# A transformer block with experts on one core: the last expert group and its norm in one pass of tokens, and the context's second-layer products moved behind it

## The chip, the cores and the metric

The kernel runs on one core of a Trainium2 chip. The metric is device microseconds of one execution. Engines: PE is TensorE (matmuls; its weight loads are listed as PEld), DVE is VectorE, ACT ScalarE, POOL GpSimd, SP SyncE (it only issues transfers here). Every time below is in us unless marked ns.

## What is computed

512 tokens of 1024 numbers pass through two blocks in float32. The first has a mixer (retention and spatial gating) and 16384 experts, of which each token takes the 16 best of each of 8 heads:

```python
expert = k1 * PEER_N_KEYS + k2
g = jax.nn.softmax(top_s.astype(jnp.float32), axis=-1).astype(hb.dtype)
ue = expert_u[expert]
act = jax.nn.gelu(jnp.einsum('td,thkd->thk', hb, ue), approximate=False) * g
ve = expert_v[expert]
return jnp.einsum('thk,thkd->td', act, ve)
...
x = x + gate2[:, None, :] * peer(h2, ...)
return rms_norm(x, final_g)
```

The second block has two layers. Each takes x and a context of 256 tokens, both normed and modulated, through one wide product; then window attention and latent attention (each over the tokens and the context), a gated convolution and a merge. Layer 0 also updates the context, `mixer_layer(..., update_ctx=(i < DEPTH_2 - 1))`; of the context, layer 1 uses only keys and values: the latent `kvlb` (256 wide), which is normed, `kr` (32), `ka` (128) and `va` (128).

## The kernel before

Every float32 product is three products of split operands (`mm3`, lines 81 to 85: high by high, low by high, high by low). So each weight tile is loaded (SP, `wr`), its high part cast on ACT (line 108, `wh`), and its low part subtracted on POOL or DVE (line 110, `wl`).

**Experts** (`experts`, line 563). For 384 tokens all experts are computed. *Up products*: for each block of 128 experts 24 products of 128x384 into `u`; the result leaves through ACT (`hb`, line 739) for memory (`hd`). Two accumulators `u` take turns. These blocks are handed out by the generator `units`, in part as filler between the steps of the routing and of the context's layers. *Down products*: 32 groups of 4 rows of 128 experts; for each row `vr` is loaded and split (`vh`, `vl`), `at` = `ht` x `gt` (line 626) is the gated activation and is split (`ah`, `al`), and 24 products of 128x384 add to eight accumulators `acc`. For the last 128 tokens only the chosen experts are computed: 128 steps, each of which gathers rows (`sg<-ur,xid` and `sg<-ev,xid`, issued by POOL), takes a dot product on DVE (line 200, via `htok`) and adds into `sacc` (line 723). `self.sparse(n)` hands these steps out by the weights S3, S4, SU and S5, which are steps per piece of dense work.

**Context** (`context`, line 1382). It runs while up products last, for both layers of the second block: the norm, the products (`cm`), in layer 0 the attention, the convolution and the merge; then the updated context is stored (`cxd`), loaded again for layer 1, normed, and its keys and values are stored to `cd[1]`.

**The last group and the norm** (`first_out`, line 903). Group 31 is computed in two halves of tokens, 256 and then 256 of which 128 come from `sacc` by a transpose (line 649). After each half: squares on ACT, sums by small products (`cs,sq`, line 928), a root on DVE, a broadcast by PE (line 159), and the modulated and split input `hh`, `hl` of layer 0.

The order of instructions within an engine is made by a scheduling layer from the program text, so code that is written in another place moves the instructions of all engines and the transfers in SP's queue.

Of the kernel before, what the change touches and what calls it, by code (L numbers as in the profile page):

```python
# [8 lines left out]
F32 = mybir.dt.float32  # L9
# [21 lines left out]
S3, S4, SU, S5 = 0.8, 0.95, 1.2, 0.82  # L31
# [24 lines left out]

class Kern:
# [23 lines left out]
    def mm3(self, ps, lh, ll, rh, rl, first, last):  # L81
        mm = self.nc.tensor.matmul
        mm(ps, lh, rh, start=first, stop=False)  # L83
        mm(ps, lh, rl, start=False, stop=False)  # L84
        mm(ps, ll, rh, start=False, stop=last)  # L85
# [167 lines left out]
    def build(self):  # L253
# [25 lines left out]
        self.cxd = dr.tile([128, 8, TC], F32, name="cxd")  # L279
        self.ud = [dr.tile([128, T], F32, name="ud%d" % k) for k in range(8)]  # L280
# [282 lines left out]
    def experts(self):  # L563
        nc, a, h = self.nc, self.a, self.h
        self.fine = ("",)
        with ExitStack() as s1:
# [21 lines left out]
            self.context(wc, pc, tick)  # L588
# [12 lines left out]
            self.last_units = True  # L601
# [5 lines left out]
            self.load(x, self.x1d)  # L607
# [3 lines left out]
            def update(c, lo, hi):  # L611
                nc.vector.scalar_tensor_tensor(x[:, c, lo:hi], acc[c][:, lo:hi], self.mod[:, 40 + c:41 + c], x[:, c, lo:hi],
                                               op0=OP.mult, op1=OP.add)
# [28 lines left out]
            def last(lo, hi):  # L642
                for c in range(8):
                    cs = slice(c * 128, (c + 1) * 128)
                    e = min(hi, TD)
                    for q, (vh, vl, ah, al) in enumerate(ops):
                        self.mm3(acc[c][:, lo:e], vh[:, cs], vl[:, cs], ah[:, lo:e], al[:, lo:e], q == 0, q == 3)
                    if hi > TD:
                        nc.tensor.transpose(acc[c][:, TD:T], self.sacc[:, cs], self.ident)
                    update(c, lo, hi)  # L650
                if hi == T and "x2" in self.dbg:
                    self.load(self.dbg["x2"], x)
# [249 lines left out]

    def first_out(self, scope, last, banks):
# [3 lines left out]
        turn = iter([banks[i] for i in (7, 6, 5, 1, 2, 3, 4, 1)])  # L907

        def stp():
            return next(turn)  # L910

# [8 lines left out]
        for hf, (lo, hi) in enumerate(HALVES):  # L920
            w = hi - lo
            last(lo, hi)
            sps = stp()
            for k in range(8):
                sq = p0.tile([128, w], F32, name="sq", tag="sq", bufs=3)
                nc.scalar.square(sq, x[:, k, lo:hi])
                for i in range(2):
                    nc.tensor.matmul(sps[:, 2 * i:2 * i + 2], sq[:, i * 128:(i + 1) * 128], cs[:, k, :],
                                     start=k == 0 and i == 0, stop=k == 7 and i == 1)
            sv = sps[:, :4].rearrange("p (i w) -> p w i", w=2)  # L930
            v = self.small.tile([128, 2, 2], F32, name="v2", tag="v2")
# [920 lines left out]
```

## Time and profile before

| | us |
|---|---|
| median of three runs | 3726.02 |
| lowest and highest | 3725.82, 3735.67 |
| the profiled execution | 3726.69 |
| its span | 3724.9 |
| PE, DVE, ACT, POOL busy | 3434.7, 2367.6, 1566.5, 1398.7 |
| last of the context's layer-0 products | 1667 |
| first down product | 1776.33 |
| first product of group 31 | 2293.51 |
| first window score of layer 0 | 2397.39 |

Busy times are sums over the whole span and overlap. The four points in time are from the trace and part the program into stages. Where a window of the trace is shown, the column PEclk is the mean granted clock of PE, with 1.00 for 2.4 GHz and 0.50 for 1.2 GHz.

### The profile page before, as it was taken

What the parts mean: (1) busy time and instruction counts of PE and PEld (TensorE: products, weight loads), DVE (VectorE), ACT (ScalarE), POOL (GpSimd) and SP (SyncE); (2) the same over time, 40 slices, a digit from 0 to 9 for tenths busy, and PEclk for the clock granted to TensorE, in tenths of its full rate; (3) what the DMA queues carried; (4) which work ended last, traced back from release to release, by engine and by line L of the source; (5) the groups of instructions that cost most, each with busy time, mean ns of one, the idle gap of its engine ahead of it and who ended that gap; (6) DMA issues with size and microseconds to landing.
All of it is one profiled execution on the core that took longest, in us unless ns stands there. A gap on an engine that the chain in (4) does not pass through costs nothing.

```text
span 3724.9 us, 54819 instructions
## 1 busy us (share of the span) xinstructions
PE 3434.7 (92%) x20315; PEld 3095.9 (83%) x20315; DVE 2367.6 (64%) x4607; ACT 1566.5 (42%) x2945; POOL 1398.7 (38%) x1170
## 2 busy tenths in 40 slices
PE   6999999978888988896999999899999988999998
PEld 5889788977788978896999999878878787787787
DVE  7876865698867666665777776444245664433554
ACT  3323233325653474643333333344346544442663
POOL 2210114452336667564222210455425335542442
PEclk9999999989999998998999998899999999999999
DMA  7667644337877757585999994322211422222123
GB/s 276 214 205 256 224 153 156 111 124 274 295 254 266 273 198 261 178 275 217 358 344 319 328 329 140 101 71 69 77 59 50 142 73 69 71 69 70 54 71 100
DMA packets 271948, 667.93 MB, mean 179 GB/s; under 512 B 25280, under 2 KB 87104, under 8 KB 268736
## 3 DMA queue, kind: packets, MB, share of 16 engines
q1 hardware_dynamic: 219248, 469.30, 37.5%
q0 software_dynamic: 36864, 134.23, 10.2%
q10 hardware_dynamic: 15568, 60.89, 4.2%
q8 instruction: 160, 2.62, 0.3%
q14 instruction: 108, 0.88, 0.1%
HBM read 601.34 MB, written 62.98 MB: 178 GB/s over the span
## 4 chain that ended last, share of the span: by engine, by line
PE 45%; DVE 4%; ACT 3%; DMA 3%; issue 2%; POOL 2%; SPq 0%; POOLq 0%; ACTq 0%; DVEq 0%
PE acc L85 5%; PE acc L84 5%; PE acc L83 5%; PE gm L83 3%; PE gm L84 3%; PE gm L85 3%; PE mm L83 3%; PE mm L85 3%; PE mm L84 3%; PE pv L1104 2%; PE tp L1074 2%; DMA vr<-ev 1%; PE sc L83 1%; PE sc L85 1%; PE sc L84 1%
## 5 line engine op out<-in xcount | busy, mean ns | idle before, releaser
L110 POOL TENSOR_TENSOR wl<-wr,wh 128x512 fp32r<-128x512 f32 (+2 forms) x348 | 483.6, 1406 | 350.6 <-ACT wh L108 325.5
L108 ACT CAST wh<-wr 128x512 fp32r<-128x512 f32 (+4 forms) x536 | 350.7, 667 | 560.7 <-PE mm L84 208.7
L83 PE MATMUL u<-hh,wh 128*128 128x384 f32 (+1 forms) x1040 | 362.6, 349 | 34.4 <-ACT hb L739 34.4
L85 PE MATMUL u<-hh,wl 128*128 128x384 f32 (+1 forms) x1040 | 360.5, 347 | 10.0 <-DVE wl L110 9.4
L84 PE MATMUL u<-hl,wh 128*128 128x384 f32 (+1 forms) x1040 | 359.8, 346 | 0.0
L84 PE MATMUL acc<-al,vh 128*128 128x384 f32 (+2 forms) x1056 | 353.4, 335 | 1.0 <-DVE al L110 1.0
L85 PE MATMUL acc<-ah,vl 128*128 128x384 f32 (+2 forms) x1056 | 353.4, 335 | 0.0
L83 PE MATMUL acc<-ah,vh 128*128 128x384 f32 (+2 forms) x1056 | 353.0, 335 | 0.0
L708 POOL DMA_INDIRECT sg<-ev,xid x128 | 158.0, 1234 | 313.5 <-DVE sacc L723 258.7
L108 ACT CAST vh<-vr 128x1024 fp32r<-128x1024 f32 x128 | 134.6, 1052 | 316.5 <-issue 140.3
L83 PE MATMUL mm<-hh,wh 128*128 128x512 f32 (+2 forms) x608 | 241.4, 401 | 8.5 <-DVE sm L419 4.2
L708 POOL DMA_INDIRECT sg<-ur,xid x128 | 145.2, 1135 | 276.9 <-DVE sg L200 260.1
L84 PE MATMUL mm<-hl,wh 128*128 128x512 f32 (+2 forms) x608 | 241.7, 398 | 7.4 <-POOL hl L110 5.4
L85 PE MATMUL mm<-hh,wl 128*128 128x512 f32 (+2 forms) x608 | 240.9, 396 | 4.4 <-DVE wl L110 4.4
L110 DVE TENSOR_TENSOR wl<-wr,wh 128x1024 fp32r<-128x1024 f32 (+4 forms) x188 | 179.5, 971 | 102.0 <-ACT wh L108 101.1
L110 DVE TENSOR_TENSOR vl<-vr,vh 128x1024 fp32r<-128x1024 f32 x128 | 159.6, 1247 | 127.3 <-ACT vh L108 124.8
L83 PEld LDWEIGHTS u<-hh,wh 128*128 128x128 f32 x1040 | 203.9, 196 | 36.6 <-ACT hb L739 35.3
L85 PEld LDWEIGHTS u<-hh,wl 128*128 128x128 f32 x1040 | 203.7, 196 | 12.9 <-DVE wl L110 12.0
L84 PEld LDWEIGHTS u<-hl,wh 128*128 128x128 f32 x1040 | 204.2, 196 | 0.3
L84 PEld LDWEIGHTS acc<-al,vh 128*128 128x128 f32 x1056 | 202.6, 192 | 1.4 <-DVE al L110 1.3
L85 PEld LDWEIGHTS acc<-ah,vl 128*128 128x128 f32 x1056 | 202.8, 192 | 0.0
L83 PEld LDWEIGHTS acc<-ah,vh 128*128 128x128 f32 x1056 | 202.5, 192 | 0.2 <-ACT hb L739 0.2
(723 smaller groups left out, 9936.9 us busy)
## 6 DMA issues: line engine op xcount, KB each, us to landing
wr<-eu SPq DMA_DIRECT2D x256, 256.0 KB
vr<-ev SPq DMA_DIRECT2D x128, 512.0 KB
wm<-wmod SPq DMA_DIRECT2D x88, 512.0 KB
wrc<-w SPq DMA_DIRECT2D x83, 512.0 KB
wr<-wA SPq DMA_DIRECT2D x80, 512.0 KB
wr<-w SPq DMA_DIRECT2D x156, 256.0 KB
wrg<-w SPq DMA_DIRECT2D x104, 256.0 KB
hd<-hb ACTq DMA_DIRECT2D x64, 384.0 KB
```

What stands on the lines that cost most here:

```text
L83: mm(ps, lh, rh, start=first, stop=False)
L84: mm(ps, lh, rl, start=False, stop=False)
L85: mm(ps, ll, rh, start=False, stop=last)
L108: nc.scalar.copy(hi, x)
L110: eng.tensor_tensor(lo, x, hi.bitcast(F32), op=OP.subtract)
L708: self.here(nc.gpsimd.indirect_dma_start(t, None, tabs[i], bass.IndirectOffsetOnAxis(idx[:, j:j + 1], 0)))
L1074: nc.tensor.transpose(t[:, (b - i) * 128:(b - i + 1) * 128], p[:, b * 128:(b + 1) * 128], self.ident)
L1104: nc.tensor.matmul(o[:, lo:hi], v(b), pt[k][:, b, lo:hi], start=i == 0 and k == 0, stop=i == len(parts) - 1 and k == 1)
```

## The change

The context's second layer leaves `context`: only the sums of its norm are still taken there, behind the merge, with up products between them (`unit`), and the row of roots is stored (`crd`). Its five products go into a new generator `context_last`, which `first_out` steps through. `first_out` takes group 31 in one pass over all 512 tokens. `mm3` and others keep the written order where `self.pinned` is set. The accumulators stay open from group 30 to group 31, so that the update of x behind group 30 goes. The load of x is written in the eighth group. S5 rises. The norm of layer 1's context latent moves to the window part of layer 1.

```diff
-S3, S4, SU, S5 = 0.8, 0.95, 1.2, 0.82
+S3, S4, SU, S5 = 0.8, 0.95, 1.2, 0.88
...
     def mm3(self, ps, lh, ll, rh, rl, first, last):
+        for i, (l, r) in enumerate(((lh, rh), (lh, rl), (ll, rh))):
+            ins = self.nc.tensor.matmul(ps, l, r, start=first and i == 0, stop=last and i == 2)
+            if self.pinned:
+                self.here(ins)
...
-            self.context(wc, pc, tick)
+            def unit(n=1):
+                for _ in range(n):
+                    self.sparse(SU)
+                    next(units, None)
+
+            self.context(wc, pc, tick, unit)
...
-            self.load(x, self.x1d)
...
+                if g == 8:
+                    self.load(x, self.x1d)
...
-                            self.mm3(acc[c][:, :TD], vh[:, cs], vl[:, cs], ah, al, g == 0 and q == 0, g == 30 and q == 3)
+                            self.mm3(acc[c][:, :TD], vh[:, cs], vl[:, cs], ah, al, g == 0 and q == 0, False)
                     self.sparse(S5)
-                if g == 30:
-                    for c in range(8):
-                        update(c, 0, TD)
...
+            def last(c):
+                cs = slice(c * 128, (c + 1) * 128)
+                for q, (vh, vl, ah, al) in enumerate(ops):
+                    self.mm3(acc[c][:, :TD], vh[:, cs], vl[:, cs], ah, al, False, q == 3)
+                self.here(nc.tensor.transpose(acc[c][:, TD:T], self.sacc[:, cs], self.ident))
+                nc.vector.scalar_tensor_tensor(x[:, c, :], acc[c], self.mod[:, 40 + c:41 + c], x[:, c, :], op0=OP.mult, op1=OP.add)
...
+    def context_last(self, pool, banks):
...
+        self.load(row, self.crd)
+        x = Split([scratch() for _ in range(2)])
+        for i, t in enumerate(x.tiles):
+            self.load(t, self.cxd[:, 4 * i:4 * i + 4, :])
...
+        yield
+        for i, n in enumerate(("kvlb0", "kvlb1", "va", "ka", "kr")):
+            w, ps = self.win(ws, l, n), banks[i]
+            c = 32 if n == "kr" else 128
+            self.fm(ps[:c, :TC], w, 0, c, h, 0, TC)
...
+            nc.scalar.copy(o, ps[:c, :TC])
+            self.store(d, o)
+            yield
...
     def first_out(self, scope, last, banks):
...
+        more = self.context_last(p0, [banks[i] for i in (1, 2, 3, 4, 5, 1)])
+        next(more)
...
+        self.pinned = True
+        for c in range(8):
+            last(c)
+            sq = p0.tile([128, T], F32, name="sq", tag="sq", bufs=4)
+            nc.scalar.square(sq, x[:, c, :])
+            sqs.append(sq)
+            if c > 1:
+                stats(c - 2)
+        next(more)
+        stats(6)
+        stats(7)
...
+        r = self.rsqrt(v.rearrange("p a b -> p (a b)"), 8, "rt8")
+        next(more)
+        for i in range(4):
+            self.here(nc.tensor.matmul(banks[6][:, i * 128:(i + 1) * 128], r[:, 4 + i:5 + i].to_broadcast([128, 128]), self.ident,
+                                       start=True, stop=True))
+        for lo, hi in HALVES:
+            self.modulate(x, lo, hi, self.h, g, m[:, 0:8], p0, banks[6][:, lo:hi])
+        for _ in more:
+            pass
+        self.pinned = False
...
-            for l in range(2):
+            for l in range(1):
...
                     self.store(self.cxd, x)
+                    self.last_units = True
+                    acc = sp.tile([128, TC], F32, name="sqa", tag="z", bufs=1)
+                    nc.scalar.square(acc, x[:, 0, :])
...
+                    unit(4)
+                    sps = tp()
+                    with self.tc.issue_after(self.pe_last()):
+                        self.col_add(sps, acc, 2, True, True)
+                    y = self.rstd_of(sps, 2, D)
+                    unit(2)
+                    bps = tp()
+                    with self.tc.issue_after(self.pe_last()):
+                        self.bcast(bps, y, 2)
...
+                    self.store(self.crd, row)
...
+            if l:
+                bps = self.rstd_rows([cx[:, i, :] for i in range(2)], 2, 2, gp, gm, (("z", 1), ("sz", 2)))
+                for i in range(2):
+                    nc.vector.scalar_tensor_tensor(cx[:, i, :], cx[:, i, :], self.v_("g_kva_2")[:, 2 * l + i:2 * l + i + 1], bps,
+                                                   op0=OP.mult, op1=OP.mult)
```

**PE at the end of the context's layer 0.** `cm` are the context's products, `u` the up products, `ones,sqa` the sums of a norm and `rs2y` its broadcast. Before, at the norm of the merge:

```order
L85 MATMUL u<-hh,wl 128x384
L83 MATMUL u<-hh,wh 128x384
L150 MATMUL ct<-ones,sqa 128x1 x2
L84 MATMUL u<-hl,wh 128x384
L85 MATMUL u<-hh,wl 128x384
```

In the changed program, at the same norm:

```order
L95 MATMUL cm<-cl,whc 128x256
L95 MATMUL cm<-ch,wlc 128x256
L162 MATMUL ct<-ones,sqa 128x1 x2
L171 MATMUL ct<-c_ident,rs2y 128x128 x2
L95 MATMUL u<-hh,wh 128x384
L95 MATMUL u<-hl,wh 128x384
L95 MATMUL u<-hh,wl 128x384
```

Before, 16 up products stand ahead of this norm's sums and 13 between them and the broadcast; now the norm follows the last `cm` directly, and the up products come after it.

**ACT at the end of the up products.** `wh` are casts of up weights, `hb` the results of up blocks, `vh` and `ah` the first operands of the down products. Before:

```order
L108 CAST ah<-at 128x384
L108 CAST vh<-vr 128x1024
L739 ACTIVATE hb<-u 128x384
L108 CAST vh<-vr 128x1024 x2
L108 CAST wh<-wr 128x512 x2
L739 ACTIVATE hb<-u 128x384
L108 CAST wh<-wr 128x512
L78 DMA hd_96<-hb 128x768
L108 CAST wh<-wr 128x512
L108 CAST ah<-at 128x384
L108 CAST vh<-vr 128x1024
L108 CAST wh<-wr 128x512
```

Now:

```order
L120 CAST wh<-wr 128x512
L120 CAST ah<-at 128x384 x2
L120 CAST vh<-vr 128x1024
L745 ACTIVATE hb<-u 128x384
L90 DMA hd_96<-hb 128x768
L120 CAST vh<-vr 128x1024 x2
L745 ACTIVATE hb<-u 128x384
L120 CAST ah<-at 128x384
L120 CAST vh<-vr 128x1024
L120 CAST ah<-at 128x384
L745 ACTIVATE hb<-u 128x384
```

The casts `vh` and `ah` stand among the last casts of up weights before and behind all of those now; three `hb` follow the first `vh` now.

**SP's queue in the same place.** `wr<-eu` are up weights, `gt`, `ht` and `vr` the inputs of the down products. Before:

```order
L75 DMA gt<-gd 128x12x128
L75 DMA ht<-hd_81 128x1536
L75 DMA vr<-ev 128x1024 x3
L75 DMA wr<-eu 128x512 x4
L75 DMA vr<-ev 128x1024
L75 DMA wr<-eu 128x512 x2
L75 DMA gt<-gd 128x12x128
L75 DMA ht<-hd_81 128x1536
L75 DMA vr<-ev 128x1024 x3
L75 DMA gt<-gd 128x12x128
L75 DMA ht<-hd_82 128x1536
L75 DMA x<-x1d 128x4096
```

Now:

```order
L87 DMA wr<-eu 128x512 x16
L87 DMA gt<-gd 128x12x128
L87 DMA ht<-hd_81 128x1536
L87 DMA vr<-ev 128x1024 x3
L87 DMA gt<-gd 128x12x128
L87 DMA vr<-ev 128x1024
L87 DMA ht<-hd_81 128x1536
L87 DMA vr<-ev 128x1024 x3
L87 DMA gt<-gd 128x12x128
L87 DMA ht<-hd_82 128x1536
L87 DMA vr<-ev 128x1024
L87 DMA x<-x1d 128x4096
```

All up weights now stand ahead of the first `gt`. The load of x comes behind the eighth `vr` where it came behind the seventh.

**ACT behind the norm of `first_out`.** `hh` is the input of layer 0, `wh` casts of its weights and, now, of the context's, `kz` and `va` the context's keys and values of layer 0, `cq<-acc` the context's results of layer 1. Before, from the second half on:

```order
L936 COPY r_72<-rt4y 128x2
L195 ACTIVATE hh<-nt,md_67 128x256 x3
L1272 CAST kz_22796<-cx 64x256 x2
L1272 CAST kz_22798<-cx 64x256
L195 ACTIVATE hh<-nt,md_67 128x256
L1272 CAST kz_22798<-cx 64x256
L195 ACTIVATE hh<-nt,md_67 128x256 x2
L108 CAST va<-cx 128x2x64 x2
L108 CAST whg<-wrg 128x512 x2
L195 ACTIVATE hh<-nt,md_67 128x256 x2
L108 CAST wh<-wr 128x512 x2
```

Now, from the norm on:

```order
L207 ACTIVATE hh<-nt,md_67 128x256 x3
L120 CAST wh<-wr 128x512 x2
L207 ACTIVATE hh<-nt,md_67 128x256
L1003 COPY r_72<-rt8y 128x4
L207 ACTIVATE hh<-nt,md_67 128x256 x2
L1336 CAST kz_22618<-cx 64x256 x2
L1336 CAST kz_22620<-cx 64x256 x2
L207 ACTIVATE hh<-nt,md_67 128x256
L120 CAST wh<-wr 128x512
L207 ACTIVATE hh<-nt,md_67 128x256 x2
L944 COPY cq<-acc_17115 128x256
L120 CAST wh<-wr 128x512
```

The casts for the context's weights and the copies of its results now stand between the `hh`; two casts of 128x256 and three `hh` follow this piece before the last cast for `kr`.

## Rows read from the trace of the kernel before

**Rows 1.** PE over the whole span, the page's part 1: busy us, share, instructions.

```profile
PE 3434.7 (92%) x20315; PEld 3095.9 (83%) x20315; DVE 2367.6 (64%) x4607; ACT 1566.5 (42%) x2945; POOL 1398.7 (38%) x1170
```

**Rows 2.** Windows: length, busy PE, PEld, DVE, ACT, POOL, PEclk, DMA share, GB/s.

```profile
1200.00:1300.00 100.00, 95.91 (x670) 95.18 (x670) 66.68 (x77) 39.08 (x70) 61.20 (x46) 0.98 0.81 281
...
1674.00:1776.00 102.00, 68.08 (x377) 65.16 (x377) 59.33 (x107) 30.17 (x61) 46.45 (x40) 0.80 0.63 230
...
1740.00:1750.00 10.00, 2.48 (x12) 2.17 (x11) 7.77 (x8) 2.88 (x4) 4.78 (x4) 0.72 1.03 409
...
1776.00:1900.00 124.00, 123.05 (x708) 122.43 (x708) 90.78 (x123) 45.12 (x64) 30.95 (x28) 1.00 0.97 353
```

**Rows 3.** Chain of waits, 1600 to 1780: start, us, what.

```profile
1621.05 0.19 PE u L84
...
1628.27 0.58 PE cm L83
...
1631.77 0.20 PE u L84
...
1673.84 0.68 PE ct L159 x4
...
1687.32 6.83 DMA cx<-cxd
...
1731.39 19.93 DMA vr<-ev
...
1776.33 0.18 PE acc L83
```

**Rows 4.** Timeline of PE: start, us, line, operation.

```profile
1600.25 0.34 PE L83 MATMUL u<-hh,wh 128*128 128x384 f32 x1
...
1604.41 0.28 PE L83 MATMUL cm<-cy,whc 128*128 128x256 f32 x1
...
1604.88 0.28 PE L84 MATMUL cm<-cy,whc 128*128 128x256 f32 x1
...
2293.51 0.28 PE L83 MATMUL acc<-ah,vh 128*128 128x256 f32 x1
```

**Rows 5.** Chain of waits, 2293 to 2400.

```profile
2307.60 0.69 PE acc L928 x4
...
2397.39 0.43 PE sc L1329 x2
```

**Rows 6.** Windows in the last group and behind it.

```profile
2320.00:2333.00 13.00, 13.00 (x65) 13.00 (x64) 6.44 (x16) 2.98 (x7) 0.00 (x0) 0.50 0.01 1
...
2357.00:2397.00 40.00, 32.60 (x259) 31.92 (x258) 17.04 (x32) 16.41 (x31) 26.90 (x23) 0.91 0.35 112
```

**Rows 7.** Waits of PE, 1700 to 1776: us in total, times, longest.

```profile
PE u L83 <- ACT hb L739: 11.9, 2, 7.5
```

**Rows 8.** Timeline of DVE and of POOL, 1728 to 1742.

```profile
1734.71 3.78 DVE L200 SCALAR_TENSOR_TENSOR sg<-sg,htok 128x1024 f32<-128x1024 f32 x1 [3.19 <-DMA sg<-ur,xid]
...
1734.85 2.55 POOL L110 TENSOR_TENSOR wl<-wr,wh 128x512 fp32r<-128x512 f32 x2
```

**Rows 9.** Gather issues, the page's part 5: busy us, mean ns, idle before.

```profile
L708 POOL DMA_INDIRECT sg<-ev,xid x128 | 158.0, 1234 | 313.5 <-DVE sacc L723 258.7
```

**Rows 10.** Groups of ACT by shape, 2340 to 2360: busy us, mean ns.

```profile
L195 ACT ACTIVATE hh<-nt,md 128x256 fp32r<-128x256 f32 x8 | 3.6, 501 | 3.1 <-DVE nt L194 3.0
L1272 ACT CAST kz<-cx 64x256 fp32r<-64x256 f32 x4 | 1.6, 402 | 0.1
L108 ACT CAST whg<-wrg 128x512 fp32r<-128x512 f32 x2 | 1.1, 616 | 0.0
```

**Rows 11.** Tiles acc and sacc: ns min/median/max, first and last start.

```profile
L928 PE MATMUL acc<-cs,sq x64: 207/352/352, 2305.8 to 2343.1; 128*128 128x2 f32 x64
...
L649 PE MATMUL acc<-c_ident,sacc x8: 435/435/435, 2313.1 to 2333.4; 128*128 128x128 f32 x8
```

**Rows 12.** Waits of PE at layer 1's first norm, 3000 to 3110.

```profile
PE sc L159 <- DVE rs2y L145: 3.0, 4, 2.3
```

More of the change, by code (lines that the diff above doesn't have):

```diff
@@ L54, in run, with __init__, __getitem__ @@
             fn()
+class Split:
+    def __init__(self, tiles):
+        self.tiles, self.shape = tiles, [128, 8, TC]
+    def __getitem__(self, at):
+        p, k, s = at
+        return self.tiles[k // 4][p, k % 4, s]
 class Kern:
@@ L919, in first_out @@
         nc.vector.tensor_tensor(cs[:, :, 1], fg, fg, op=OP.mult)
[L920 to L931, printed above, removed]
-            nc.vector.tensor_scalar(out=v[:, 0, :], in0=sv[:, 0, :], scalar1=1.0 / D, scalar2=EPS, op0=OP.mult, op1=OP.add)
-            nc.vector.tensor_scalar(out=v[:, 1, :], in0=v[:, 0, :], scalar1=EPS, scalar2=None, op0=OP.mult)
-            nc.vector.scalar_tensor_tensor(v[:, 1, :], sv[:, 1, :], 1.0 / D, v[:, 1, :], op0=OP.mult, op1=OP.add)
-            r = self.rsqrt(v.rearrange("p a b -> p (a b)"), 4, "rt4")
-            nc.scalar.copy(self.r1[:, 2 * hf:2 * hf + 2], r[:, 0:2])
-            bps = stp()
-            self.bcast(bps, r[:, 2:4], 2)
-            self.modulate(x, lo, hi, self.h, g, m[:, 0:8], p0, bps[:, :w])
@@ new lines, in first_out, with stats @@
+        more = self.context_last(p0, [banks[i] for i in (1, 2, 3, 4, 5, 1)])
+        next(more)
+        sps, sqs = banks[0], []
+        def stats(k):
+            for i in range(4):
+                self.here(nc.tensor.matmul(sps[:, 2 * i:2 * i + 2], sqs[k][:, i * 128:(i + 1) * 128], cs[:, k, :],
+                                           start=k == 0 and i == 0, stop=k == 7 and i == 3))
+        self.pinned = True
[6 more added lines that the diff above has]
+                stats(c - 2)
@@ new lines, in first_out @@
+        next(more)
+        stats(6)
+        stats(7)
+        sv = sps[:, :8].rearrange("p (i w) -> p w i", w=2)
+        v = self.small.tile([128, 2, 4], F32, name="v2", tag="v2")
+        nc.vector.tensor_scalar(out=v[:, 0, :], in0=sv[:, 0, :], scalar1=1.0 / D, scalar2=EPS, op0=OP.mult, op1=OP.add)
+        nc.vector.tensor_scalar(out=v[:, 1, :], in0=v[:, 0, :], scalar1=EPS, scalar2=None, op0=OP.mult)
+        nc.vector.scalar_tensor_tensor(v[:, 1, :], sv[:, 1, :], 1.0 / D, v[:, 1, :], op0=OP.mult, op1=OP.add)
@@ new lines, in first_out @@
+        r = self.rsqrt(v.rearrange("p a b -> p (a b)"), 8, "rt8")
+        next(more)
+        for i in range(4):
+            self.here(nc.tensor.matmul(banks[6][:, i * 128:(i + 1) * 128], r[:, 4 + i:5 + i].to_broadcast([128, 128]), self.ident,
[4 more added lines that the diff above has]
+            pass
+        self.pinned = False
+        nc.scalar.copy(self.r1, r[:, 0:4])
@@ L1380, in consts2, with context @@
         nc.vector.tensor_scalar(out=self.nsink, in0=self.nsink, scalar1=-1.0, scalar2=None, op0=OP.mult)
-    def context(self, ws, pu, tick):
+    def context(self, ws, pu, tick, unit):
         nc, a = self.nc, self.a
@@ L1412, in context @@
                     x = np_.tile([128, 8, TC], F32, name="cx")
[L1413 removed]
+                    self.load(x, a["ctxT"])
                     self.norm_mod(x, 0, TC, h, g, m[:, 0:8], np_, tp)
@@ L1462, in context @@
                     self.store(self.cxd, x)
+                    self.last_units = True
+                    acc = sp.tile([128, TC], F32, name="sqa", tag="z", bufs=1)
+                    nc.scalar.square(acc, x[:, 0, :])
+                    for k in range(1, 8):
+                        sq = sp.tile([128, TC], F32, name="sq", tag="sz", bufs=2)
+                        nc.scalar.square(sq, x[:, k, :])
+                        nc.vector.tensor_tensor(acc, acc, sq, op=OP.add)
+                    unit(4)
[7 more added lines that the diff above has]
+                        self.bcast(bps, y, 2)
+                    row = sp.tile([128, TC], F32, name="crow", tag="cs", bufs=2)
+                    nc.scalar.copy(row, bps[:, :TC])
+                    self.store(self.crd, row)
                     if "cl0" in self.dbg:
@@ L1579, in rest @@
             self.load(cx, self.cd[l][:, 0:2, :])
+            if l:
+                bps = self.rstd_rows([cx[:, i, :] for i in range(2)], 2, 2, gp, gm, (("z", 1), ("sz", 2)))
+                for i in range(2):
+                    nc.vector.scalar_tensor_tensor(cx[:, i, :], cx[:, i, :], self.v_("g_kva_2")[:, 2 * l + i:2 * l + i + 1], bps,
+                                                   op0=OP.mult, op1=OP.mult)
             self.split(kv[0][:, :, T:TX], kv[1][:, :, T:TX], cx)
```

55 lines of the change are left out of this document (30 added, 25 removed).

## The prediction

> **What bounds the kernel now.** I read the busy times first. TensorE (PE) is busy for 3434.7 us of a span of 3724.9, 92% [rows 1], so a change pays only where PE stands still, runs at its lower clock or does work that can be dropped. The change drops no product, so I looked for the other two in the stretches that it touches.
>
> The table of windows shows both. From 1200 to 1300 us PE works 95.91 of 100 us, and from 1776 to 1900, in the down products, 123.05 of 124 at a granted clock of 1.00 [rows 2]. Between them, from 1674 to 1776, it works 68.08 of 102 us at 0.80, and in one window there 2.48 of 10 us [rows 2]; 0.50 in that column is the lower of its two clocks, 1.2 GHz, and 1.00 the upper, 2.4. The chain of waits says why [rows 3]. The context's last layer-0 products are followed by the merge's norm (broadcast at 1673.84); the context is stored, fetched back (1687.32, 6.83 us) and normed, its layer-1 products run, and only then come the last 192 up products. These wait for transfers, one of experts for 19.93 us, and the first down product starts at 1776.33.
>
> The second stretch is the last group. Its products start at 2293.51 [rows 4] and the first window score at 2397.39 [rows 5], 103.9 us later. PE looks busy there, 13.00 of 13 us, but runs at 0.50 while it works through 128-column products [rows 6].
>
> **Term 1, the end of the context.** The program order keeps the number of up products: 264 after the context's last layer-0 product in both, of which the changed kernel puts none beside the merge's own norm. That norm now stands alone on PE: it ends where its broadcast ends, 1673.84 + 0.68 = 1674.5 [rows 3], since the sums that it waits for come from VectorE (DVE), which does the same as before. Before, 29 up products stood beside it, 29 x 0.173 = 5.0 us; now this is a hole. Then 264 products follow in one block, with the new context norm inside it, behind 96 and 144 of them, so that its chain is covered.
>
> Twenty-four such products took 1604.41 - 1600.25 = 4.16 us, 0.173 each [rows 4], so the block is 11 x 4.16 = 45.8. After a hole of 7.0 us (1621.2 to 1628.27) the products ran at half speed until 1631.77 [rows 3]: 3.5 us, half of it lost, 1.8. That makes 1674.5 + 45.8 + 1.8 = 1722.1 if nothing starves the block.
>
> Something will, a little. The order puts the first expert casts (ah, vh) on ScalarE (ACT) ahead of the last three hb, which free the accumulators of the up products; the DVE product at that feeds ah stands behind gathered rows. Before, where the order is alike, PE waited for hb twice, 11.9 us in all [rows 7]. All loads of up weights now precede the first gt, ht and vr on SyncE's (SP) queue, so those three are asked for once the last of these has a free buffer, four or five blocks of 24 ahead of the end, near 1704. Due in the 55 us are 16 wr of 0.25 MB, 13 gathers and 4 vr of 0.5, 4 gt and ht of 0.75, five hd of 0.38 and the context, 1.0: 18.4 MB or 335 GB/s, below the 409 that the chip showed [rows 2]. So I take not 11.9 but 5, between 0 (all lands in time) and 24 (rival 1): the down products start at 1727.1. Gain 1776.3 - 1727.1 = **49.2**, bounds 30 to 54.
>
> DVE and GpSimd (POOL) have to fit into that stretch. POOL has 16 wl adds of 2.55 / 2, 4 cx adds of half their width and 13 gather issues of 1.23 [rows 8, 9], 39 us; DVE, at the share of the stretch now (59.33 of 102 [rows 2]) on 60 us, 35. From 1200 to 1300 they were busy 66.68 and 61.20 of 100 us and PE still did 95.91 [rows 2], so 74 in 60 us should pass. But a DVE product took 3.78 while POOL's two adds of 2.55 ran; 3.78 - 2.55 = 1.23 is what it has alone [rows 8]. The Trainium skill, "SBUF — State Buffer", section "Who interferes with whom", says that the port pair which these two engines share is an exclusive lock, the loser blocked for the whole instruction. By that, with gather issues left out, about 23 + 35 = 58 us would stand one behind the other from 1667, up to 1725, and the last product's 4.16 us on PE after them would put the start at 1729 and the sum 2 us higher. The 3.78 agrees with it; the window with 95.91 shows that PE can be fed all the same.
>
> **The down products.** 124 rows of experts at 24 x 0.173 = 4.16 are 516, which is what they take now (1776.3 to 2293.5). The order moves the load of x by one vr load only: it stands behind the eighth vr instead of the seventh, so it is not fetched in the eighth group but where it is now. I cost it at nothing; its cover is the experts' rows already loaded, of which the changed kernel holds fewer (rival 3). The larger S5 (0.88 for 0.82) brings gathers 7% faster, at 353 GB/s against the 409 shown [rows 2]: nothing. The eight updates of x behind group 30 are DVE's, beside PE: nothing.
>
> **Term 2, the last group.** Per step, from 2293.51: 96 products at 0.173, 16.7 (before, 96 of 256 columns and 96 of 128, the second lot at a clock of 0.50 [rows 6]); 8 transposes at half of 0.435 [rows 11], 1.7; the sums for the norm, 64 records [rows 11] that took 0.173 each at the low clock (0.69 for four [rows 5]), at the full one half of that, 5.6; kvlb0 and kvlb1, 48 products at 0.1175 (four from 1604.41 to 1604.88 [rows 4]), 5.6; waits for the last expert row and the root, 0.9; broadcast 0.7. That is 31.2.
>
> Then the two halves are modulated, while PE has va, ka and kr. By the order ACT has to do 12 hh (0.45), 4 wide and 2 narrow weight casts (0.62 and about half), 4 kz (0.40), two va and 3 copies of a kz's size before kr's second half [rows 10]: 5.4 + 2.5 + 0.6 + 1.6 + 0.6 + 1.2 = 11.9 us; with DVE's first step, POOL's adds and the last 12 products, 14.8 from the broadcast to the first layer-0 product. Then 344 products at 0.1175, 40.4, and stalls as now: 40.0 - 32.6 = 7.4 between 2357 and 2397 [rows 6]. Sum 93.8 against 103.9, gain **10.1**. Bounds 2 (the clock falls again and the products for va to kr take double) to 19 (the casts do not hold up PE and the stalls go).
>
> **Term 3, layer 1.** The second layer's window part gets a norm of the context's latent: two sums, a root, a broadcast, four DVE operations. A root of that kind made PE wait 2.3 at most nearby [rows 12]. It stands beside other products, so I take **+1**, between -3 (the scores start earlier, as the two products after them moved) and +5.
>
> Sum: 3726.69 - 49.2 - 10.1 + 1 = 3668.4 for an execution like the profiled one; the median is 0.67 lower, so **3668**.
>
> **Rivals.**
> 1. *The up products starve.* Both waits for hb come back (11.9), with some 3.5 us at the low clock after each, as after the hole before 1628.27, and the loads, one of which took 19.93 us [rows 3], land some 4 us late; or POOL and DVE work one after the other, 74 us from 1667. Both put the start at 1741 to 1745: 3682 to 3687. For it: the order on ACT, and 409 GB/s at which transfers already ran. Against: fewer transfers are due than before. Chance 0.15.
> 2. *The last group gains nothing*: the clock drops in the holes between va, ka and kr. Then 3678. Against it: no 128-column products are left. Chance 0.10.
> 3. *Slower.* Four rows of experts are loaded at the start of the down products where seven were, and x (2 MB, 5 us at 409 GB/s) goes ahead of the ninth. If PE then runs dry row after row, the clock falls to 0.50, where a row takes 8.3 instead of 4.16. The gains of 58 are used up after 14 rows so run, and 17 make it slower by over 0.3%: 3738. Against it: the window after 1776 has 353 GB/s and PE at 1.00; a row asks for 0.5 MB each 4.16 us. Chance 0.03.
> 4. *The change does not do what it says*: for the load of x this is so, by the order, and is in the sum.
>
> **How the numbers follow.** The forecast with its bounds, 3655 to 3681, has 0.65; rival 1 0.15, rival 2 0.10, better than forecast (all lands in time, term 2 at its upper end) 0.04, rival 3 0.03, small mishaps together 0.03. The range takes in rivals 1 and 2 and some of the better case: 3647 to 3698. About 0.3%, 11 us, is what a measurement of this kernel tells from no change. Faster by more 0.94, within it 0.03, slower 0.03.
>
> **What would show it.** In the new profile: the first down product near 1727; 264 up products at 0.173 with one hole, ahead of them; a granted clock near 1.0 from 1680 and in the last group; 94 us from the end of group 30 to the first score; layer 1 within some us. I am wrong if PE waits for hb by more than 10 us, if down products run with holes, or if the clock of the last group stays at 0.5.

## The result, and the profile after

| | before | changed |
|---|---|---|
| median of five runs | 3726.02 | 3703.34 |
| lowest and highest | 3718.18, 3735.67 | 3694.28, 3706.51 |
| ratio, 95% interval | | 0.9926 [0.9911, 0.9942] |
| span of the profiled execution | 3724.9 | 3701.6 |

The change is faster by 0.7%: some 28 us by the ratio, 22.7 us between the medians and 23.3 us between the two profiled executions. The forecast was 58 us, with a time of 3668 in a range of 3647 to 3698: the sign came out, the time lies outside. By stages of the two profiled executions:

| stage | before | forecast | changed |
|---|---|---|---|
| start to the context's last layer-0 product | 1666.7 | 1666.7 | 1664.6 |
| from there to the first product of group 31 | 626.8 | 577.6 | 597.5 |
| from there to the first window score | 103.9 | 93.8 | 104.6 |
| from there to layer 1's last norm sum | 645.4 | 645.4 | 645.6 |
| from there to the end | 682.3 | 683.3 | 689.3 |

So 20 us are missing between the context's last product and group 31, 11 in the last group and 6 in layer 1. Of the 20, one half lies ahead of the first down product (at 1734.65, 70.0 us behind the context's last product, forecast 60.4), the other half in the first rows of the down products. The page of the profile has PE at 92% as before [rows 1], busy for 19.5 us less:

```profile
PE 3415.2 (92%) x20219; PEld 3074.3 (83%) x20219; DVE 2369.2 (64%) x4572; ACT 1564.2 (42%) x2940; POOL 1407.8 (38%) x1178
```

The windows of the changed kernel around the start of the down products (length, busy PE, PEld, DVE, ACT, POOL, PEclk, DMA share, GB/s), to be read against [rows 2]:

```profile
1670.00:1680.00 10.00, 10.00 (x47) 10.00 (x47) 5.40 (x15) 2.79 (x7) 5.04 (x6) 0.76 0.03 10
1680.00:1690.00 10.00, 10.00 (x61) 10.00 (x60) 9.37 (x9) 4.03 (x10) 7.97 (x7) 1.00 0.99 341
1690.00:1700.00 10.00, 8.53 (x47) 7.58 (x45) 8.05 (x14) 2.63 (x6) 7.84 (x7) 1.00 1.03 409
1700.00:1710.00 10.00, 9.27 (x53) 8.99 (x54) 9.93 (x13) 4.02 (x9) 7.93 (x5) 1.00 0.49 164
1710.00:1720.00 10.00, 8.82 (x48) 7.88 (x47) 4.17 (x5) 2.22 (x4) 9.37 (x8) 1.00 0.91 294
1720.00:1730.00 10.00, 1.84 (x7) 1.62 (x6) 6.62 (x9) 2.99 (x5) 8.62 (x7) 0.63 1.02 407
1730.00:1740.00 10.00, 5.51 (x25) 5.19 (x23) 4.71 (x6) 2.42 (x4) 1.68 (x1) 0.84 1.06 387
1740.00:1750.00 10.00, 5.71 (x18) 5.71 (x19) 3.78 (x6) 1.85 (x3) 1.01 (x1) 0.51 0.94 337
1750.00:1760.00 10.00, 10.00 (x60) 10.00 (x59) 6.80 (x10) 4.15 (x6) 2.02 (x2) 1.00 1.04 405
```

The block of up products runs, as forecast, from 1670.6 on, but with gaps from 1690; from 1720 to 1745 PE stands still two thirds of the time; from 1750 the down products run without a hole. Where the waits come from, on PE (total, times, longest), on SP and on ACT (start, us, operation, idle time before and its releaser):

```profile
PE u L95 <- ACT hb L745: 9.1, 3, 8.2
PE acc L95 <- ACT hb L745: 8.8, 1, 8.8
```

```profile
1664.09 49.20 SPq L87 DMA_DIRECT2D wr<-eu  x14
1713.45 0.39 SPq L87 DMA_DIRECT2D gt<-gd  x1
1713.89 1.11 SPq L87 DMA_DIRECT2D ht<-hd  x1
1715.04 2.17 SPq L87 DMA_DIRECT2D vr<-ev  x3
```

```profile
1700.32 1.93 ACT L120 CAST wh<-wr 128x512 fp32r<-128x512 f32 x3 [5.39 <-DMA wr<-eu]
...
1708.67 0.62 ACT L120 CAST wh<-wr 128x512 fp32r<-128x512 f32 x1 [5.25 <-DMA wr<-eu]
...
1714.72 0.62 ACT L120 CAST wh<-wr 128x512 fp32r<-128x512 f32 x1 [4.13 <-DMA wr<-eu]
...
1726.89 1.04 ACT L120 CAST vh<-vr 128x1024 fp32r<-128x1024 f32 x1 [0.94 <-DMA vr<-ev]
1727.84 0.48 ACT L745 ACTIVATE hb<-u 128x384 f32<-128x384 f32 x1
...
1742.39 1.04 ACT L120 CAST vh<-vr 128x1024 fp32r<-128x1024 f32 x1 [7.08 <-DMA vr<-ev]
1743.35 0.51 ACT L120 CAST ah<-at 128x384 fp32r<-128x384 f32 x1
1743.76 0.48 ACT L745 ACTIVATE hb<-u 128x384 f32<-128x384 f32 x1
```

These are the waits of rival 1: PE waits for hb, 17.9 us in all against the 11.9 of [rows 7] (the prediction named 10 as a sign of being wrong), the long ones behind a vh that waits for its transfer. But two things stand ahead of them. SP needed 49.20 us to hand out the up weights, so gt, ht and vr were asked for at 1713 and not near 1704; and the up weights themselves arrived late, 4 to 5 us of waiting before each pair of casts.

Late does not mean slow in each case. SP asks for the next up weight when POOL's subtraction `wl` has freed a buffer. For the wait that ends at 1708.67 these are the rows of POOL and of SP, and below them a row of POOL from a run without gathers there (d_gath0, see the experiments):

```profile
1701.88 1.69 POOL L714 DMA_INDIRECT sg<-ev,xid  x1 [3.14 <-DVE sacc L729]
1703.59 3.75 POOL L122 TENSOR_TENSOR wl<-wr,wh 128x512 fp32r<-128x512 f32 x2
```

```profile
1705.13 0.33 SPq L87 DMA_DIRECT2D wr<-eu  x1
```

```profile
1699.37 2.55 POOL L122 TENSOR_TENSOR wl<-wr,wh 128x512 fp32r<-128x512 f32 x2 [1.05 <-ACT wh L120]
```

POOL waits 3.14 us for DVE's sum before it can issue a gather; the subtraction behind the gather starts 2.7 us after its cast has ended; SP asks for the load as soon as the first of the two is done, at 1705.13, and it lands 3.4 us later. Of the 16 subtractions of the block, 15 start 1.5 to 7.6 us behind their casts; without gathers all start within 1.2. The loads asked for at 1684.44 and 1695.03 took 7.2 and 5.2 us, but those from 1705 on 2.6 to 3.9, and without gathers they take 2.5 to 5.4. So ACT's waits of 1708.67 and 1714.72 are late requests: while it waits for 5.25 us, the window from 1700 to 1710 moves only 164 GB/s. The one of 1700.32 is both, a slow transfer that was also asked for late.

In the last group two steps show. DVE's root chain is cut in two by a cast of the window mask that waits for its load, and the broadcast behind it and what follows run at the low clock; the weights of va and ka are cast among the hh (timeline of DVE, of PE and of ACT, then two windows):

```profile
2291.66 0.17 DVE L152 TENSOR_SCALAR rt8i<-v 128x8 int32<-128x8 int32 x1
2293.99 0.29 DVE L1639 CAST bmask<-bm 128x256 bf16<-128x256 f32 x1 [2.16 <-DMA bm<-bmask]
2294.20 0.17 DVE L153 TENSOR_SCALAR rt8y<-rt8i 128x8 int32<-128x8 int32 x1
```

```profile
2296.22 2.07 PE L996 MATMUL acc<-c_ident,rt8y 128*128 128x128 f32 x8 [2.27 <-DVE rt8y L157]
2300.72 0.80 PE L95 MATMUL acc<-cq,wh 128*128 128x256 f32 x2 [2.42 <-ACT wh L120]
...
2307.83 0.51 PE L95 MATMUL acc<-cq,wh 128*128 128x256 f32 x2 [0.88 <-ACT wh L120]
```

```profile
2298.85 1.31 ACT L207 ACTIVATE hh<-nt,md 128x256 fp32r<-128x256 f32 x3 [4.48 <-DVE nt L206]
2300.06 1.12 ACT L120 CAST wh<-wr 128x512 fp32r<-128x512 f32 x2
...
2307.16 0.62 ACT L120 CAST wh<-wr 128x512 fp32r<-128x512 f32 x1 [1.34 <-DMA wr<-w]
```

```profile
2286.00:2296.00 10.00, 7.96 (x68) 7.75 (x67) 2.81 (x15) 1.38 (x3) 0.00 (x0) 1.00 0.87 328
2296.00:2306.00 10.00, 6.51 (x27) 5.92 (x28) 7.83 (x17) 5.67 (x14) 4.59 (x4) 0.50 0.16 51
```

### The profile page after: what moved, and what is told of

Read it like the earlier page. It is cut to its first block, busy times and chain, and to the rows that moved or that the text cites. A ratio compares the mean times of both kernels' runs of the same rounds, so it can differ in the third digit from the quotient of the medians.

```text
span 3701.6 us, 54609 instructions
## 1 busy us (share of the span) xinstructions
PE 3415.2 (92%) x20219; PEld 3074.3 (83%) x20219; DVE 2369.2 (64%) x4572; ACT 1564.2 (42%) x2940; POOL 1407.8 (38%) x1178
## 3 DMA queue, kind: packets, MB, share of 16 engines
q0 software_dynamic: 36864, 134.23, 10.1%
## 4 chain that ended last, share of the span: by engine, by line
PE 65%; DVE 13%; DMA 7%; issue 7%; ACT 5%; POOL 3%; SPq 0%; POOLq 0%; ACTq 0%; DVEq 0%
PE mm L95 16%; PE acc L95 12%; PE gm L95 10%; PE u L95 8%; PE cm L95 4%; PE uq L95 2%; PE sc L95 2%; PE pv L1168 2%; DMA wr<-eu 2%; PE tp L1138 2%; PE pv L95 2%; PE tp L95 1%; DVE wm L212 1%; DVE wl L122 1%; POOL wl L122 1%
## 5 line engine op out<-in xcount | busy, mean ns | idle before, releaser
L122 POOL TENSOR_TENSOR wl<-wr,wh 128x512 fp32r<-128x512 f32 (+3 forms) x358 | 499.0, 1411 | 452.3 <-ACT wh L120 437.6
L120 ACT CAST wh<-wr 128x512 fp32r<-128x512 f32 (+3 forms) x546 | 355.8, 665 | 576.2 <-PE mm L95 201.5
L95 PE MATMUL acc<-ah,vh 128*128 128x384 f32 x1024 | 343.9, 336 | 8.8 <-ACT hb L745 8.8
L95 PE MATMUL acc<-al,vh 128*128 128x384 f32 x1024 | 343.3, 335 | 0.9 <-DVE al L122 0.9
L95 PE MATMUL acc<-ah,vl 128*128 128x384 f32 x1024 | 343.2, 335 | 0.0
L122 DVE TENSOR_TENSOR wl<-wr,wh 128x1024 fp32r<-128x1024 f32 (+4 forms) x188 | 179.5, 972 | 101.2 <-ACT wh L120 100.1
L729 DVE SCALAR_TENSOR_TENSOR sacc<-sg,wts,sacc 128x1024 f32<-128x1024 f32 x128 | 189.3, 1479 | 22.5 <-DMA sg<-ev,xid 19.0
L95 PEld LDWEIGHTS acc<-ah,vh 128*128 128x128 f32 x1024 | 193.1, 189 | 9.3 <-ACT hb L745 9.1
L95 PEld LDWEIGHTS acc<-al,vh 128*128 128x128 f32 x1024 | 193.1, 189 | 1.1 <-DVE al L122 1.1
```

The source lines that it names most:

```text
L95: ins = self.nc.tensor.matmul(ps, l, r, start=first and i == 0, stop=last and i == 2)
L120: nc.scalar.copy(hi, x)
L122: eng.tensor_tensor(lo, x, hi.bitcast(F32), op=OP.subtract)
L729: self.here(nc.vector.scalar_tensor_tensor(acc, t, wts[:, j:j + 1], acc, op0=OP.mult, op1=OP.add))
```

## The experiments

The same code upstream of the context's last layer-0 product took 1664.6 to 1677.2 us in the profiled executions of this study, so a point in time alone would mislead. The times of the table are from several sessions (the median of the kernel before was 3726.02 beside the changed kernel, 3735.24 beside d_gath0, g_all and g_all_sp), so they are compared as ratios to the kernel before. All runs are read by stages: A from that product to the first transpose of the gathered part in group 31 (3.4 us behind the group's first product, so that the forecast for A is 581.0); B from there to the first window score; C from layer 1's last norm sum to the end.

| run | A | B | C | us | runs |
|---|---|---|---|---|---|
| changed kernel | 600.9 | 101.2 | 689.3 | 3703.34 | 5 |
| a_act | 598.1 | 102.0 | 685.8 | 3701.73 | 1 |
| a_actsp | 600.4 | 101.6 | 685.9 | 3703.26 | 1 |
| a_gath | 587.7 | 100.9 | 684.6 | 3696.97 | 1 |
| bc_mask_nonorm | 601.7 | 97.7 | 681.3 | 3699.44 | 1 |
| d_gathact | 586.4 | 99.2 | 687.1 | 3688.59 | 1 |
| d_gath0act | 581.7 | 99.9 | 684.5 | 3684.79 | 1 |
| d_gath0 | 582.2 | 101.2 | 685.6 | 3689.98 | 4 |
| f_pre_late_mask | 602.3 | 96.9 | 684.9 | 3697.52 | 1 |
| e_noctx | 600.9 | 86.6 | 686.4 | 3689.88 | 1 |
| g_all | 582.1 | 97.4 | 681.4 | 3681.16 | 4 |
| g_all_sp | 585.1 | 98.6 | 684.6 | 3689.14 | 4 |

### What holds up the start of the down products

Three theories: (1) the order on ACT, hb behind vh and ah; (2) the first expert rows are asked for too late; (3) the gathers beside the last up blocks crowd the transfers. The rows of POOL above speak for a fourth, which got no run of its own: (4) the steps of the gathered part hold up POOL and DVE, and with them the subtractions that free the weights' buffers. The first run takes away (1); `pin` keeps a cast at its place in the text:

```diff
-        nc.scalar.copy(hi, x)
+        ins = nc.scalar.copy(hi, x)
+        if pin:
+            self.here(ins)
...
-                    self.split(vh, vl, raw, pool=False)
+                    self.split(vh, vl, raw, pool=False, pin=g == 0)
...
-                    self.split(ah, al, at, pool=False)
+                    self.split(ah, al, at, pool=False, pin=g == 0)
...
                 if g == 8:
-                    self.load(x, self.x1d)
+                    self.here(nc.sync.dma_start(x, self.x1d))
```

> Edit: the casts vh and ah of the first group are pinned behind the last hb on ACT, and the load of x is pinned to its place in the text. Marker: the first transpose of the gathered part in group 31, at 2265.5 us in the changed kernel. Theory 1 (PE waits because the last three hb stand behind casts that wait for transfers): the last up blocks run on at once and the marker comes 12 to 16 us earlier, 2250 to 2253. Theory 2 (the transfers of the first expert rows are asked for too late, whatever the order on ACT): PE waits for vr in place of hb, marker 0 to 5 earlier. Theory 3 (gathers crowd the transfers): as theory 2.

Stage A fell by 2.8. The up products were done 9.5 us sooner, 60.4 behind the context's last product instead of 69.9, but PE then waited for the operands of the down products instead:

```profile
PE acc L95 <- ACT ah L120: 12.0, 2, 6.2
...
PE u L95 <- ACT hb L747: 1.7, 2, 1.4
```

Theory 1 alone falls: the wait changed its name. x was here asked for at 1851.90 instead of 1753.28, and no hole came of it.

The second run adds an early request, pinned on SP ahead of the last six up weights (`keep` pins the loads that are written under it):

```diff
-            first = inputs(0)
-            for _ in units:
+            for i in range(2):
+                self.sparse(SU)
+                next(units)
+            self.keep = True
+            first = inputs(0)
+            rows = [row(n) for n in range(3)]
+            for _ in units:
                 self.sparse(SU)
+            self.keep = False
```

> Edit: as the run before, and the first gt, ht and three vr are asked for ahead of the last six up weights. Theory 1: as without it, marker near 2251. Theory 2: a good part of the loss is this one, marker 2241 to 2246, 20 to 25 us earlier than in the changed kernel. Theory 3: the up weights behind them now come later in their place, marker 2250 or later.

Stage A 600.4, no gain: PE now waited 7.4 us for the cast of up weights, and ACT for their transfers, which came behind the requests:

```profile
1725.01 2.63 ACT L123 CAST wh<-wr 128x512 fp32r<-128x512 f32 x4 [6.22 <-DMA wr<-eu]
```

Who is served first only moved the wait, as theory 3 expected. The third run changes two constants:

```diff
-S3, S4, SU, S5 = 0.8, 0.95, 1.2, 0.88
+S3, S4, SU, S5 = 0.8, 0.95, 0.4, 0.95
```

> Edit: SU 0.4 for 1.2 (a third of the gathers beside the last up products), S5 0.95 for 0.88. Theory 3: 24 up products take 4.2 to 4.4 us again in place of 5.2, vr lands within 6 us in place of 12, marker 15 to 20 us earlier. Theories 1 and 2: 0 to 5 earlier.

Stage A fell by 13.2, nearly what theory 3 asked for and far above the 5 of theories 1 and 2. The first vr still took 9.4 us to land, though (asked for at 1716.68, its cast could start at 1726.1), and not 6. The edit takes away whole steps of the gathered part, their transfers, their issues on POOL and their work on DVE, so it can't tell theory 3 from theory 4. Two more doses, with the pinned casts, and then the constants alone (SU 0, S5 0.99):

> Edit: fewer gathers beside the last up products (SU 0.4, S5 0.95) and the casts of the first group pinned behind the last hb, the load of x in its place in the text. Measure: from the context's last layer-0 product to the first transpose of the gathered part in group 31: 600.9 us in the changed kernel, 587.7 with fewer gathers alone, 598.1 with the pinned casts alone. With fewer gathers PE still waited 9.7 us for hb. Theory 1+3 (those waits are the order on ACT, and what made the pinned casts fail alone was DVE's at behind gathers): 578 to 581. Theory 2 (late asking): PE waits for vr or ah instead, 585 to 588.

> Edit: as the run before with no gathers at all beside the last eleven blocks (SU 0, S5 0.99). Theory 3 with more to come from the gathers that were left: 575 to 578. If the third of them did no harm, or the gathers now crowd the down products: 579 or more.

> Edit: the changed kernel with SU 0 and S5 0.99 alone. If the order on ACT costs nothing once the gathers are gone: product to transpose 581 to 584, as with the pinned casts. If both are needed: 586 to 592, with PE waiting for hb by 5 to 10 us.

With SU 0.4 the pinned casts brought 1.3 us: the waits went from hb to ah and al, as theory 2 has it there. With SU 0 stage A is 581.7 with them and 582.2 without, so the order on ACT is worth nothing there, and 18.7 of the missing 19.9 us go with the gathers' steps. The last third of them did harm too, some 5 us, less than the 8 to 11 that was expected: by the recorded ranges 581.7 counts as no harm, or as gathers that now crowd the down products, and the second was not looked into. Groups of ACT over 35 us of the block of up products, in the changed kernel and without gathers (busy us, mean ns, idle before):

```profile
L120 ACT CAST wh<-wr 128x512 fp32r<-128x512 f32 x12 | 7.4, 619 | 21.6 <-DMA wr<-eu 21.5
```

```profile
L120 ACT CAST wh<-wr 128x512 fp32r<-128x512 f32 x14 | 8.5, 616 | 13.6 <-PE u L95 13.6
```

In the first ACT waits for weights, in the second for PE to free their buffers: a block held up by late weights, and one that PE paces. The windows without gathers have no gap, and one wait of PE is left, at the start of the down products:

```profile
1690.00:1700.00 10.00, 10.00 (x61) 10.00 (x60) 2.92 (x8) 5.49 (x13) 5.86 (x6) 1.00 0.89 309
1700.00:1710.00 10.00, 10.00 (x61) 10.00 (x60) 3.19 (x10) 3.50 (x8) 6.33 (x6) 1.00 0.52 173
1710.00:1720.00 10.00, 10.00 (x60) 10.00 (x59) 0.81 (x4) 3.08 (x7) 6.18 (x6) 1.00 0.89 289
```

```profile
PE acc L95 <- ACT hb L745: 7.4, 1, 7.4
```

Did the gathers cost as much before the change? The same constant in the kernel before, with S5 0.88:

```diff
-S3, S4, SU, S5 = 0.8, 0.95, 1.2, 0.82
+S3, S4, SU, S5 = 0.8, 0.95, 0.4, 0.88
```

> Edit: the kernel before with the gathers' pace alone changed (SU 0.4, S5 0.88). From the context's last layer-0 product to the first down product there are 109.5 us before. If the gathers beside the last up blocks held that stage up before as they do in the changed kernel: 93 to 99, time 10 to 16 us lower than before. If the context's second layer between them is what took the time: 105 to 110, time within 5.

From the context's last layer-0 product (1677.2 there) to the first down product (1774.7) it took 97.5 us in place of 109.5: 12 us, inside the range for gathers. The time fell by less than the 10 to 16 us expected: ratio 0.998 [0.9963, 0.9996], some 7 us; up to the first transpose stage A fell by 7.3, from 646.3 to 639.0, so part of the 12 was lost again in the down products. So the gathers held up that stage before as well. The context's second layer, which the change moved away, still leaves its hole in this run:

```profile
1709.17 0.99 PE L150 MATMUL ct<-ones,sqa 128*128 128x1 f32 x4 [16.84 <-DVE sqa L177]
```

### The last group and layer 1

One kernel with two edits in places apart:

```diff
-        nc.vector.tensor_copy(self.bmask, bm)
+        nc.gpsimd.tensor_copy(self.bmask, bm)
...
-            if l:
+            if False:
                 bps = self.rstd_rows([cx[:, i, :] for i in range(2)], 2, 2, gp, gm, (("z", 1), ("sz", 2)))
```

> Edits in two places apart: the cast of the window mask goes from DVE to POOL, and layer 1's norm of the context latent is left out (the latent enters unnormed). Place 1: if the root chain of the last norm is held by that cast, which waits for its load in the middle of it, the first window score comes 3 to 4 us sooner after the marker (101.2 us in the changed kernel); if something else ends last there, 0 to 1. Place 2: from layer 1's first norm sum to the end there are 689.7 us, 682.6 before the change. If the norm itself costs the difference, 682 to 685; if it is the new order of what stands around the scores, 688 to 691.

Stage B fell by 3.5, as expected for the mask (over the runs of the table that keep the context's products it is 99.2 to 102.0 with the cast on DVE and 96.9 to 98.6 with it on POOL); the broadcast starts without a wait and at the full clock, 1.16 us in place of 2.07:

```profile
2304.07 1.16 PE L996 MATMUL acc<-c_ident,rt8y 128*128 128x128 f32 x8
```

Stage C was 681.3. It scatters, though: eight executions that share its code with the changed kernel have 684.5 to 689.3, 686.2 in the mean, and the kernel before has 682.3, with fewer gathers 683.0. So by this one run the norm costs some 5 us, against the kernel before 3 to 4, and the 689.3 of the profiled execution is the upper end. Next, the weights of va with buffers of their own, and the norm moved behind the gates of the window part:

```diff
-            w, ps = self.win(ws, l, n), banks[i]
+            w, ps = self.win((pool, 2, 1, "x") if n == "va" else ws, l, n), banks[i]
...
             yield from self.gates_of(ws, l, 2, True, mt, yc, gp, fill, h, T)
+            cx = gp.tile([128, 2, TC], F32, name="cl", tag="u", bufs=2)
+            self.load(cx, self.cd[l][:, 0:2, :])
+            if l:
+                bps = self.rstd_rows([cx[:, i, :] for i in range(2)], 2, 2, gp, fill, (("z", 1), ("sz", 2)))
...
+            self.split(kv[0][:, :, T:TX], kv[1][:, :, T:TX], cx)
```

> Edits: buffers of its own for the weights of va, so that they are fetched and split ahead of the last group; the mask's cast on POOL; layer 1's norm of the latent moved behind the gates of the window part. Transpose to first window score: 101.2 us in the changed kernel, 97.7 with the mask's cast on POOL alone. Theory A (the casts and loads of va, ka and kr, one behind the other, hold up PE behind the broadcast): 91 to 95. Theory B (ACT's and DVE's work on the two halves ends last there): 97 to 98. Last norm sum of layer 1 to the end: 684.6 to 689.3 in four runs with the norm, 681.3 without it; if the place of the norm costs that, 681 to 683, if its work does, 684 or more.

Stage B 96.9, so 0.8 less than the mask's cast alone: theory A falls. The stretch from the broadcast to the first layer-0 product did get shorter, 16.3 us (17.0 with the mask's cast alone), and kept the full clock. In the changed kernel and in this run:

```profile
2298.30:2317.00 18.70, 13.27 (x74) 11.96 (x75) 16.73 (x33) 12.38 (x31) 10.41 (x11) 0.70 0.21 68
```

```profile
2298.80:2315.00 16.20, 9.95 (x74) 8.08 (x72) 15.11 (x33) 12.81 (x33) 6.95 (x8) 1.00 0.27 80
```

What it gained there was in part lost behind it, 51.0 us to the first score in place of 49.7. Stage C 684.9: the place inside layer 1 matters little, if at all. Then the five products left out:

```diff
...
-            w, ps = self.win(ws, l, n), banks[i]
             c = 32 if n == "kr" else 128
-            self.fm(ps[:c, :TC], w, 0, c, h, 0, TC)
...
-            nc.scalar.copy(o, ps[:c, :TC])
             self.store(d, o)
```

> Edit: the five products of the context, the loads and casts of their weights and the copies of their results are left out of the last group (the normed context is stored in their place), nothing else. They hold 14.1 us of PE at the upper clock. Transpose to first window score: theory A (they hold up the layer by their chain of weights): 101.2 falls by 18 to 25 us. Theory B (their time is their PE time, or less where the halves are modulated): by 6 to 14 us.

Stage B fell by 14.6, just over theory B's range and below theory A's. Their PE time at the upper clock is 14.1: on balance they are neither hidden nor do they hold up more than themselves. Without them PE waits 6.0 us for the root, which they cover:

```profile
PE acc L992 <- DVE rt8y L157: 6.0, 1, 6.0
```

### A version that beats both

SU 0 and S5 0.99, the pinned casts, the mask on POOL, and the norm of layer 1's latent done behind layer 0's window part, where the latent is stored back:

```diff
             yield from self.gates_of(ws, l, 2, True, mt, yc, gp, fill, h, T)
+            if l == 0:
+                cx = gp.tile([128, 2, TC], F32, name="cl", tag="u", bufs=2)
+                self.load(cx, self.cd[1][:, 0:2, :])
+                bps = self.rstd_rows([cx[:, i, :] for i in range(2)], 2, 2, gp, fill, (("z", 1), ("sz", 2)))
...
+                self.store(self.cd[1][:, 0:2, :], cx)
```

> Edit: no gathers beside the last up blocks (SU 0, S5 0.99), the first group's casts pinned behind the last hb, the mask's cast on POOL, layer 1's norm of the latent done behind layer 0's window part and stored back. Product to transpose 581 to 583 as with the first two alone, transpose to score 97 to 98, last norm sum to end 681 to 683 if the norm's cost is its place at the start of layer 1 (684 or more if not). Time by the parts: 3677 to 3683, ratio 0.987 to 0.989.

Ratio to the kernel before 0.9869 [0.9844, 0.9895], below the changed kernel's 0.9926 [0.9911, 0.9942]; stages A and B as expected, C at 681.4 in the one that was profiled. The constants alone (d_gath0) have 0.9885 [0.9857, 0.9913], so the intervals of these two overlap, and what the other three edits add is not shown by the time; the interval of d_gath0 also just touches that of the changed kernel. With the early requests on SP as well:

> Edit: as the run before, and gt, ht and three vr are asked for ahead of the last four up weights. Theory 2 for what is left of the waits at the start of the down products (5 us for ah and al): product to transpose 576 to 579. If the up weights behind them now come late: 582 or more.

Stage A 585.1, ratio 0.9883 [0.9861, 0.9904]: no gain; PE waited 3.7 us for the cast of up weights again. Stage C is 684.6 here, with the same code in layer 1 as the 681.4 before it, and layer 0, where the norm now stands, took 647.0 us up to layer 1's last norm sum in both, against 645.6 in the changed kernel. So it stays open whether moving the norm there gained anything.

## Why the prediction was wrong

**The hole at the merge's norm and the block behind it** were right: the hole, then 24 products in 4.2 us, and with few gathers or none the block ended 53.2 to 54.3 us behind the context's last product (d_gathact, d_gath0act, d_gath0 and g_all), where the working gives 1722.1 - 1666.7 = 55.4.

**"So I take not 11.9 but 5" was the step that failed**, the price of waiting in term 1. From the context's last product to group 31 it took 597.5 us where 577.6 were forecast, 19.9 more. The 5 was taken from a mean, 18.4 MB in 55 us or 335 GB/s against 409 shown; POOL's and DVE's 74 us in 60 were weighed by a mean too. A mean does not tell what waits. The up weights have buffers for two blocks, and a buffer is asked for again when POOL's subtraction is done, so PE feels a load that takes long, or a subtraction that comes late, two blocks later. Beside the gathers' steps both came: loads of 7.2 and 5.2 us, and subtractions 1.5 to 7.6 us behind their casts. The block took 1734.5 - 1670.6 = 64 us instead of 48, and since all weights stand ahead on SP, "near 1704" became 1713; then the first rows of the down products waited too. Shown by the runs is that the loss goes with the gathers' steps (18.7 of the 19.9 us); how much of it is their transfers, and how much their work on POOL and DVE, was only read from rows, and no run parts the two.

The run without gathers gives stage A 582.2 against 581.0 forecast. That it is so close is luck in part: there the first down product comes 53.4 us behind the context's last, where the sum has 60.4, and the rows of the down products up to group 31 take 525.4, with the wait of 7.4 for hb, where the sum has 517.2.

**Rival 1 named the waits, not their cause.** It put them down to the order on ACT; taking that order away brought 2.8 us, and 0.5 without gathers. The waits for hb are where late weights and rows come out. Its other parts, loads that land some 4 us late, or POOL and DVE one after the other, are nearer to what the rows show. Its price, 14 to 19 us, is nearly the 19.9. Its 0.15 was too low for a case that [rows 7] showed in the kernel before.

**"So 74 in 60 us should pass"** looked at busy time as well. The subtractions themselves became only a little longer, 1.46 us each against 1.29 without gathers, for 15 of them 2.4 us in all. The rows show what the sum left out, that they stand behind gathers on POOL, and behind gathers that wait for DVE.

**Term 2** was 10.1 and came out as -0.7. The way to the broadcast's end took 2298.3 - 2262.1 = 36.2 where 31.2 were forecast. The cut root chain and the slow broadcast, which no step had, are some 3 of these 5, by the run with the mask elsewhere; the rest is open. The stretch from the broadcast to the first layer-0 product was forecast with 14.8 and took 2317.0 - 2298.3 = 18.7; the stretch behind it with 47.8 and took 49.7. Rival 2's reason, the clock, holds in part: 1.00 until the broadcast, 0.50 from 2296 to 2306, 0.70 over the 18.7 us. Without their inner holes the 24 products of va took some 5.2 us and those of ka some 4.7, where 24 x 0.1175 are 2.8; that makes an estimate of 4 us for the low clock. With buffers for va the clock stayed at 1.00 and the stretch took 16.3. The prediction's "no 128-column products are left" did not help: the clock was low from the broadcast on, after a wait of 2.27 us, and again in ka's products, after the next holes. What decides the rest of this stretch was not settled.

**Term 3** was +1 and is some 2 to 5, within its bounds: stage C is 686.2 in the mean with the norm there, and 681.3 to 684.6 without it. The 7.0 between the two profiled executions is the upper end of that scatter. [rows 12] gave the wait for one root; what else the norm holds up was not looked into.

**Load of x, S5**: right. **The down products** run at 10.00 of 10 from 1750 on; their 516 of before are 2293.5 - 1776.3 = 517.2.

## What to carry to other kernels

Where work is packed closer, ask of each stream of loads how many buffers it has, how soon a load must land, and what stands on its engine ahead of the instruction that frees the buffer, and not whether the mean of bytes or of busy time fits. Work whose time can be chosen (here the steps with gathers) belongs where PE's operands are already there. Where a wait is taken away and another engine's name takes its place, as in the run with the pinned casts, look upstream of both; a run that removes the suspect tells whether it is the cause, but not by which of its parts.

## What was not expected of the hardware

A small DVE operation can be held for several instructions of POOL: a product of 128x16 elements, 0.17 us as the median of eight, took 5.09 us while POOL ran four subtractions in a row (one instruction each, merged into one row here):

```profile
1693.68 5.09 DVE L727 TENSOR_TENSOR wts<-wts,gates 128x16 f32<-128x16 f32 x1 [1.68 <-issue]
```

```profile
1693.72 5.01 POOL L122 TENSOR_TENSOR wl<-wr,wh 128x512 fp32r<-128x512 f32 x4
```

The rule that the prediction quotes, from the Trainium skill, "SBUF — State Buffer", section "Who interferes with whom", has the loser blocked for the whole of the other's instruction; here the wait spans four of them. It stands on the path of the late requests above: behind this product on DVE come the rest of a root and, from 1700.33 to 1701.61, the sum for which POOL's gather at 1701.88 waits. How much of the loss goes back to it is not shown.
